# A rotary embedding on one core: the first piece's row 0 is stored by a DMA of its own

## The chip, the cores and the metric

The kernel runs on 1 core of one Trainium2 chip. The metric is device time in microseconds; for a kernel the median of several runs is given. All times below that carry a place in the execution are counted from the start of the profiled span.

## The reference

```python
def setup_inputs():
    batch, seq_len, num_heads, head_dim = (8, 2048, 16, 64)
    return {'x': np.random.randn(batch, seq_len, num_heads, head_dim).astype(np.float32), 'cos': np.random.randn(seq_len, head_dim // 2).astype(np.float32), 'sin': np.random.randn(seq_len, head_dim // 2).astype(np.float32)}

def reference(x, cos, sin):
    x1 = x[..., :head_dim // 2].copy()
    x2 = x[..., head_dim // 2:].copy()
    cos = cos[None, :, None, :].copy()
    sin = sin[None, :, None, :].copy()
    out1 = x1 * cos - x2 * sin
    out2 = x1 * sin + x2 * cos
    return np.concatenate([out1, out2], axis=-1).astype(np.float32)
```

Each head's 64 numbers are two halves of 32; the output is the input times cos plus the input with its halves exchanged times (-sin, sin). The input x is 67.1 MB of float32, the output as much, cos and sin 0.26 MB each. So at least 134.7 MB go through the DMA engines.

## The kernel before

A sequence position of one batch is a row of 16 x 64 floats, 4096 bytes. The 2048 positions of a batch are laid out with 16 consecutive ones to a partition (J = 16), and a piece is 8 of these rows (R = 8) on all 128 partitions: 32,768 contiguous bytes a partition, 4 MB in all. There are 16 pieces, two to a batch. They live in one SBUF tile, `buf`, with five slots (NBUF = 5); piece p uses slot p % 5 and is changed in place.

For a stretch of rows of a piece, `rotate` issues: a product v = x with exchanged halves times the signed sin (VectorE, L80), a product x = x times cos in place (VectorE, L93), and the sum x = x + v in place (GpSimd, L99). In the last piece a part of the sum is done on VectorE (L87 and L96). `in_order` keeps VectorE's instructions in program order. Most pieces are two stretches of four rows, so two additions of 128x4096. Piece 0 is cut finer: rows 0 to 2, 2 to 4, and 4 to 8, so that its three additions on GpSimd are of 128x2048, 128x2048 and 128x4096.

All loads are issued by SyncE (SP) at L52 (cos and sin at L101 and L103), all stores by ScalarE (ACT) at L55. Piece 0 is loaded in three DMAs (1, 1 and 2 MB), every other piece in one of 4 MB. Pieces 0 to 4 are loaded at the start; the load of piece p + 5 is issued when the store of piece p has landed, as it goes into the same slot. Pieces 0 to 14 leave by one store of 4 MB each, the last piece by three of 2, 1 and 1 MB. A store waits for the additions of its rows. ScalarE does nothing else besides three small copies of sin and cos into PSUM at the start.

Every DMA is spread over 16 DMA engines, 8 partitions to each, and each partition's contiguous bytes are one packet: a 4 MB load or store is 8 packets of 32,768 bytes on each engine, and one of 4 bytes that signals its completion. Loads and stores are two queues (q1 and q10 in the profile) that share the same 16 engines. The compiler gives the DMAs eight completion semaphores in rotation, and a DMA whose semaphore is in use by an earlier one waits for that one to land.

Of the kernel before, what the change touches and what calls it, by code (L numbers as in the profile page):

```python
# [1 line left out]

# [4 lines left out]


@with_exitstack  # L10
def kernel(
    ctx: ExitStack,
    tc: tile.TileContext,
    x: bass.AP,
    cos: bass.AP,
    sin: bass.AP,
    out: bass.AP,
):
    nc = tc.nc
    f32 = mybir.dt.float32  # L20

    B, S, H, D = x.shape
    Dh = D // 2
    P = nc.NUM_PARTITIONS
    J = S // P
    R = 8
    C = 4
    HALVES = J // R
    NP = B * HALVES
    NBUF = 5  # L30

    const_pool = ctx.enter_context(tc.tile_pool(name="rope_const", bufs=1))
    io_pool = ctx.enter_context(tc.tile_pool(name="rope_io", bufs=1))
    tmp_pool = ctx.enter_context(tc.tile_pool(name="rope_tmp", bufs=2))
    ps_pool = ctx.enter_context(tc.tile_pool(name="rope_ps", bufs=1, space=bass.MemoryType.PSUM))
    psv_pool = ctx.enter_context(tc.tile_pool(name="rope_psv", bufs=1, space=bass.MemoryType.PSUM))

    sin_f = const_pool.tile([P, J, Dh], f32)
    cos_f = const_pool.tile([P, J, Dh], f32)
    sin_p = ps_pool.tile([P, J, D], f32)  # L40
    cos_p = ps_pool.tile([P, J, Dh], f32)
    buf = io_pool.tile([P, NBUF, R, H, D], f32)

    def rows(t, p, r0, r1):
        b, j0 = p // HALVES, (p % HALVES) * R
        return t[b].rearrange("(p j) h d -> p j (h d)", j=J)[:, j0 + r0 : j0 + r1, :].rearrange("p j f -> p (j f)")

    def flat(t):
        return t.rearrange("p j h d -> p (j h d)")

    def load(p, r0=0, r1=R):
        nc.sync.dma_start(out=flat(buf[:, p % NBUF, r0:r1, :, :]), in_=rows(x, p, r0, r1))  # L52

    def store(p, r0=0, r1=R):
        nc.scalar.dma_start(out=rows(out, p, r0, r1), in_=flat(buf[:, p % NBUF, r0:r1, :, :]))  # L55

    order = []

    def in_order(op):
        if order:  # L60
            tc.add_manual_dep(
                op.ins,
                order[-1].ins.name,
                mybir.DependencyInfo(mybir.DependencyClass.NoSync, mybir.DependencyReason.DATA),
                reason="order of the vector engine",
            )
        order.append(op)

    def rotate(p, r0, r1, on_vector=0):
        n = r1 - r0  # L70
        j0 = (p % HALVES) * R + r0
        js = slice(j0, j0 + n)
        xt = buf[:, p % NBUF, r0:r1, :, :]
        rev = xt.rearrange("p j h (e d) -> p j h e d", e=2)[:, :, :, ::-1, :]
        sin_b = sin_p[:, js, :].rearrange("p j (e d) -> p j e d", e=2).unsqueeze(2).to_broadcast([P, n, H, 2, Dh])
        cos_b = cos_p[:, js, :].unsqueeze(2).to_broadcast([P, n, 2 * H, Dh])
        m = n - on_vector
        if m:
            v = tmp_pool.tile([P, C, H, D], f32)
            in_order(nc.vector.tensor_mul(  # L80
                out=v[:, 0:m, :, :].rearrange("p j h (e d) -> p j h e d", e=2),
                in0=rev[:, 0:m, :, :, :],
                in1=sin_b[:, 0:m, :, :, :],
            ))
        if on_vector:
            w = psv_pool.tile([P, 2, H, D], f32)
            in_order(nc.vector.tensor_mul(  # L87
                out=w[:, 0:on_vector, :, :].rearrange("p j h (e d) -> p j h e d", e=2),
                in0=rev[:, m:n, :, :, :],
                in1=sin_b[:, m:n, :, :, :],  # L90
            ))
        xw = xt.rearrange("p j h (e d) -> p j (h e) d", d=Dh)
        in_order(nc.vector.tensor_mul(out=xw, in0=xw, in1=cos_b))  # L93
        if on_vector:
            xa = flat(xt[:, m:n, :, :])
            in_order(nc.vector.tensor_add(out=xa, in0=xa, in1=flat(w[:, 0:on_vector, :, :])))  # L96
        if m:
            xa = flat(xt[:, 0:m, :, :])
            nc.gpsimd.tensor_add(out=xa, in0=xa, in1=flat(v[:, 0:m, :, :]))  # L99

    nc.sync.dma_start(out=sin_f, in_=sin.rearrange("(p j) d -> p j d", j=J))  # L101
    load(0, 0, 2)
    nc.sync.dma_start(out=cos_f, in_=cos.rearrange("(p j) d -> p j d", j=J))  # L103
    load(0, 2, 4)
    load(0, 4, R)
    for p in range(1, NBUF):
        load(p)
    nc.scalar.copy(out=sin_p[:, :, Dh:D], in_=sin_f)  # L108
    nc.scalar.mul(out=sin_p[:, :, 0:Dh], in_=sin_f, mul=-1.0)  # L109
    nc.scalar.copy(out=cos_p, in_=cos_f)  # L110
    for p in range(NP):
        if p == 0:
            rotate(p, 0, 2)
            rotate(p, 2, 4)
            rotate(p, 4, 8)
            store(p)
        elif p == NP - 1:
            rotate(p, 0, 4, 1)
            store(p, 0, 4)
            rotate(p, 4, 6, 1)  # L120
            store(p, 4, 6)
            rotate(p, 6, 8, 2)
            store(p, 6, 8)
        else:
            rotate(p, 0, 4)
            rotate(p, 4, 8)
            store(p)
        if p + NBUF < NP:
            load(p + NBUF)


# [1 line left out]
_INS = ['x', 'cos', 'sin']  # L133
_OUTS = [((8, 2048, 16, 64), 'float32')]


# [23 lines left out]
```

## Time and profile before

| | us |
|---|---|
| median of 3 runs | 318.33 |
| lowest and highest | 318.25, 318.38 |
| the profiled execution | 318.49 |
| its span, first to last instruction | 316.7 |

| engine | busy us | share of the span |
|---|---|---|
| VectorE | 287.5 | 91% |
| GpSimd | 274.8 | 87% |
| ScalarE | 3.1 | 1% |

| DMA | what it is |
|---|---|
| read from HBM | 67.63 MB |
| written to HBM | 67.11 MB |
| mean over the span | 425 GB/s |

The profiled execution's time is 1.8 us longer than its span: that is what lies before the first and behind the last instruction. A row of the table by stretches that is used below gives, for a stretch of the span, how long each engine was busy, and for the DMA packets that *started* in it the share of the 16 engines' time that they took and their bytes over the stretch's length. The trace has, besides, a record of every DMA packet: queue, start, duration, size.

### The profile page before, as it was taken

How to read it: one execution, taken by the hardware profiler on the slowest of the kernel's cores; microseconds unless marked ns; L12 is line 12 of the kernel's file. 1: busy time of each engine (PE TensorE's matmuls, PEld its weight loads, DVE VectorE, ACT ScalarE, POOL GpSimd, SP SyncE). 2: the span in 40 equal slices, each digit the busy share in tenths (PEclk: the TensorE clock that was granted, in tenths of full speed). 3: DMA queues.
4: the chain of work that ended last, by engine and by line, in shares of the span. 5: the costliest groups of instructions: out<-in, count | busy, mean ns of one | idle time of the engine just before them, and what ended most of it. 6: DMA issues, size and time to landing. Idle time of an engine off the chain costs nothing.

```text
span 316.7 us, 272 instructions
## 1 busy us (share of the span) xinstructions
DVE 287.5 (91%) x73; ACT 3.1 (1%) x4; POOL 274.8 (87%) x37
## 2 busy tenths in 40 slices
DVE  2999999999999999999999999799697997979960
ACT  3000000000000000000000000000000000000000
POOL 0659999999999999999999999989969899797900
DMA  7999999999999999999999999999999999999997
GB/s 301 460 430 447 348 464 426 435 451 410 459 401 464 397 464 397 464 414 447 435 426 459 401 464 397 464 398 459 410 451 435 426 451 410 455 406 460 406 428 300
DMA packets 5474, 134.76 MB, mean 425 GB/s; under 512 B 608, under 2 KB 608, under 8 KB 864
## 3 DMA queue, kind: packets, MB, share of 16 engines
q1 hardware_dynamic: 2880, 67.63, 50.0%
q10 hardware_dynamic: 2592, 67.11, 49.1%
q14 instruction: 2, 0.02, 0.0%
HBM read 67.63 MB, written 67.11 MB: 425 GB/s over the span
## 4 chain that ended last, share of the span: by engine, by line
POOL 39%; DMA 32%; DVE 21%; issue 3%; SPq 0%; POOLq 0%; DVEq 0%
POOL buf L99 39%; DMA buf<-in_x_dram 22%; DMA out_dram<-buf 11%; DVE buf L93 10%; DVE v L80 8%; DVE buf L96 1%; DVE w L87 1%; SPq L101 0%; POOLq L99 0%; DVEq L80 0%; SPq L52 0%
## 5 line engine op out<-in xcount | busy, mean ns | idle before, releaser
L99 POOL TENSOR_TENSOR buf<-buf,v 128x4096 f32<-128x4096 f32 (+3 forms) x33 | 274.6, 8335 | 26.2 <-DVE buf L93 25.8
L80 DVE TENSOR_TENSOR v<-buf,sin_p 128x4096 f32<-128x4096 f32 (+3 forms) x33 | 137.3, 4161 | 17.3 <-DMA buf<-in_x_dram 15.7
L93 DVE TENSOR_TENSOR buf<-buf,cos_p 128x4096 f32<-128x4096 f32 (+1 forms) x34 | 141.8, 4170 | 1.2
L96 DVE TENSOR_TENSOR buf<-buf,w 128x1024 f32<-128x1024 f32 (+1 forms) x3 | 4.7, 1575 | 0.1
L87 DVE TENSOR_TENSOR w<-buf,sin_p 128x1024 f32<-128x1024 f32 (+1 forms) x3 | 4.7, 1579 | 0.0
L108 ACT ACT_TABLE_LOAD x1 | 1.3, 1283 | 0.7 <-PEq L144 0.7
L110 ACT COPY cos_p<-cos_f 128x512 f32<-128x512 f32 x1 | 0.6, 590 | 2.1 <-DMA cos_f<-in_cos_dram 2.1
L108 ACT COPY sin_p<-sin_f 128x512 f32<-128x512 f32 x1 | 0.6, 589 | 1.4 <-DMA sin_f<-in_sin_dram 1.4
L109 ACT ACTIVATE sin_p<-sin_f 128x512 f32<-128x512 f32 x1 | 0.6, 601 | 0.0
L144 POOL MEMSET const-float32-0.0<- 128x1 f32 x1 | 0.1, 98 | 0.2 <-issue 0.2
L144 POOL MEMSET const-bfloat16-1.0<- 128x1 bf16 x1 | 0.1, 101 | 0.0
L144 POOL MEMSET const-uint8-127<- 128x1 uint8 x1 | 0.1, 101 | 0.0
L144 POOL MEMSET const-float32-1.0<- 128x1 f32 x1 | 0.1, 98 | 0.0
## 6 DMA issues: line engine op xcount, KB each, us to landing
buf<-in_x_dram SPq DMA_DIRECT2D x15, 4096.0 KB, 31.4
out_dram<-buf ACTq DMA_DIRECT2D x15, 4096.0 KB, 31.4
buf<-in_x_dram SPq DMA_DIRECT2D x2, 1024.0 KB, 6.0
buf<-in_x_dram SPq DMA_DIRECT2D x1, 2048.0 KB, 11.5
out_dram<-buf ACTq DMA_DIRECT2D x1, 2048.0 KB, 11.9
out_dram<-buf ACTq DMA_DIRECT2D x2, 1024.0 KB, 10.8
sin_f<-in_sin_dram SPq DMA_DIRECT2D x1, 256.0 KB, 2.7
cos_f<-in_cos_dram SPq DMA_DIRECT2D x1, 256.0 KB, 5.1
```

The costliest lines, as they stand in the source:

```text
L80: in_order(nc.vector.tensor_mul(out=v[:, 0:m, :, :].rearrange("p j h (e d) -> p j h e d", e=2), in0=rev[:, 0:m, :, :, :], in1=sin_b[:, 0:m ...
L87: in_order(nc.vector.tensor_mul(out=w[:, 0:on_vector, :, :].rearrange("p j h (e d) -> p j h e d", e=2), in0=rev[:, m:n, :, :, :], in1=sin_ ...
L93: in_order(nc.vector.tensor_mul(out=xw, in0=xw, in1=cos_b))
L96: in_order(nc.vector.tensor_add(out=xa, in0=xa, in1=flat(w[:, 0:on_vector, :, :])))
L99: nc.gpsimd.tensor_add(out=xa, in0=xa, in1=flat(v[:, 0:m, :, :]))
L108: nc.scalar.copy(out=sin_p[:, :, Dh:D], in_=sin_f)
L109: nc.scalar.mul(out=sin_p[:, :, 0:Dh], in_=sin_f, mul=-1.0)
L110: nc.scalar.copy(out=cos_p, in_=cos_f)
L144: nc = _bacc.Bacc("TRN2", target_bir_lowering=False, num_devices=1)
```

## The change

The store of piece 0 is cut in two. Row 0 (4096 bytes a partition, 512 KB in all) is stored by a DMA of its own that is issued behind the first `rotate`, which has added rows 0 and 1. Rows 1 to 8 (28,672 bytes a partition, 3.5 MB) follow where the store of the whole piece was.

```diff
     for p in range(NP):
         if p == 0:
             rotate(p, 0, 2)
+            store(p, 0, 1)
             rotate(p, 2, 4)
             rotate(p, 4, 8)
-            store(p)
+            store(p, 1, 8)
         elif p == NP - 1:
             rotate(p, 0, 4, 1)
             store(p, 0, 4)
```

The computation, the loads and all other stores are as they were. There is one DMA more on ScalarE's queue, 19 rather than 18.

## The prediction

> **What bounds the kernel now.** I read the share of each engine first, then the DMA rows, then the chain of waits, and then a table by stretches.
>
> ```profile
> DVE 287.5 (91%) x73; ACT 3.1 (1%) x4; POOL 274.8 (87%) x37
> DMA  7999999999999999999999999999999999999997
> GB/s 301 460 430 447 348 464 426 435 451 410 459 401 464 397 464 397 464 414 447 435 426 459 401 464 397 464 398 459 410 451 435 426 451 410 455 406 460 406 428 300
> q1 hardware_dynamic: 2880, 67.63, 50.0%
> q10 hardware_dynamic: 2592, 67.11, 49.1%
> POOL 39%; DMA 32%; DVE 21%; issue 3%; SPq 0%; POOLq 0%; DVEq 0%
> ```
>
> The chain names GpSimd first, but it only walks back along one possible path. The DMA rows say what cannot be shortened: the 16 engines are busy in every slice but the first and the last, and the packets of the two queues took 50.0 + 49.1 = 99.1% of the span. The rates jump between slices because a slice is credited with packets that start in it, and a round of 16 packets of 32 KB is half a MB.
>
> The packet records give the account. A packet of 2, 8, 16 and 32 KB takes 0.084, 0.309, 0.611 and 1.213 us: nearly 0.008 us and 27.2 GB/s. One engine has 240 packets of 32 KB, 16 of 16 KB, 32 of 8 KB and 16 of 2 KB: 291.1 + 9.8 + 9.9 + 1.3 = 312.1 us. The first packet starts at 1.74 and the last ends at 315.42, 313.7 us apart. So each engine loses only 1.6 us between its first and last packet, and I looked for where:
>
> ```profile
> 33.90:35.10 1.20, 1.20 (x1) 0.00 (x0) 1.20 (x1) 1.00 1.01 437
> 35.10:36.60 1.50, 1.50 (x1) 0.00 (x0) 1.50 (x1) 1.00 1.03 350
> 36.60:38.35 1.75, 1.72 (x2) 0.00 (x0) 1.75 (x1) 1.00 0.97 300
> 38.35:39.50 1.15, 1.15 (x1) 0.00 (x0) 1.15 (x1) 1.00 1.05 456
> 39.50:40.70 1.20, 1.20 (x1) 0.00 (x0) 1.20 (x1) 1.00 1.01 437
> ```
>
> Each row holds one packet of 32 KB on each engine (rate x length is 0.525 MB, 16 packets), so share x length is its mean duration: 1.21, then 1.545 and 1.70, then 1.21 again. The first two slow ones are loads; the next is the first packet of the first store. By the packet records the two cost 0.85 us an engine with their gaps (0.74 to 1.01 on the 16). They follow on this:
>
> ```profile
> 10.90 9.04 POOL L99 TENSOR_TENSOR buf<-buf,v 128x2048 f32<-128x2048 f32 x2 [10.46 <-DVE buf L93]
> ...
> 24.41 17.69 POOL L99 TENSOR_TENSOR buf<-buf,v 128x4096 f32<-128x4096 f32 x2 [4.46 <-DVE buf L93]
> 28.70 4.42 DVE L93 TENSOR_TENSOR buf<-buf,cos_p 128x4096 f32<-128x4096 f32 x1
> 33.31 0.38 ACTq L55 DMA_DIRECT2D out_dram<-buf  x1
> ```
>
> So: store queue empty, loads streaming, the first store is issued at 33.31, 1.8 us later the loads slow, and 5.1 us after the issue the store's first packet starts. From there on the queues alternate packet by packet, neither runs empty until the loads end at 281.4, and no later store or load issue shows such a loss. I call it the start-up of the store queue. The kernel is bound by the DMA engines' packet time, start-ups included.
>
> **The change, part by part.**
>
> *Bytes and packets.* The bytes are the same; so the early row gains nothing by itself: the engines are full with loads at that time, and 512 KB moved forward push loads back by as much. On each engine 8 packets of 32 KB become 8 of 4 and 8 of 28 KB. From 0.008 us and 27.2 GB/s: 0.159 + 1.062 - 1.213 = 0.008 us, by 8 is 0.064; with one more completion packet (0.009 us in the records) +0.07 us. All of it is on the bound.
>
> *The store queue starts twice.* The early store is issued when the first addition ends: GpSimd starts at 10.90 and its two additions of 128x2048 take 4.5 us each, so at about 15.46. By the same delays as before its first packet starts at about 15.46 + 5.1 = 20.6. Eight packets of 4 KB alternate with loads, (0.159 + 1.213) x 8 = 11.0, so it is done at about 31.6. The next store's descriptors are there at 33.31 + 1.8 = 35.1. So the queue is empty for about 3.5 us with loads streaming, as it was before its first start, and starts again. The trace does not show a second start. Bounds: 0 if the loss belongs to the first use, 0.85 us if to each start; below nothing if the small first store makes both cheaper (a rival). Nearest row: at 210.41 one engine had a packet of 8 KB of its instruction queue, empty for 200 us, between loads and stores; the load behind it took 1.747 rather than 1.213 us, 0.53 lost (in the store-only stretch, at 285.32, only 0.09). That is a queue joining a stream of loads after the program's start, with a loss of the same order. I take 0.85.
>
> *The Trainium skill.* "DMA: Bandwidth & Descriptors", Rules for kernel authors, asks for DMAs of 1 MiB and more, and its Anatomy section puts a fixed cost of about 2.0 us on each (fitted on the GpSimd path). By that the sum would be 318.33 + 2.0 = 320.3. The trace speaks against it in a stream: loads 1 and 2 land at 23.35 and 33.05, 9.70 us apart, which is 8 x 1.213.
>
> *Other engines.* The loss at about 17 to 20 us and the 4 KB packets fall on load 1, which lands at 23.35 + 0.85 + 2 x 0.159 = 24.5 rather than 23.35. VectorE starts on it at 24.25 now, and a landing reaches its waiter 0.45 us later (store 0 landed at 56.91, load 5 is issued at 57.35): it starts at about 24.95, 0.7 late. GpSimd then is 0.7 late for piece 1, and store 1 is issued at about 51.9 instead of 51.17. Its descriptors are there 1.8 us later, at 53.7; the store queue needs them when the 3.5 MB store's eight rounds are over, at 38.4 + 8 x (1.062 + 1.213) = 56.6: 2.9 us of cover. Without it loads 3 and 4 would fill the engines, and a third start-up would be the loss. At the end, the last store is issued at 306.2, and its packets start only when the one before it is done, at 312.97: 4.9 us of cover behind the 1.8 of an issue. So lateness of compute costs nothing.
>
> *Queues and semaphores.* On ScalarE's queue the early store stands ahead of the 3.5 MB store, which waits longer anyway. The semaphore rotation shifts by one: loads 3 and 4 now wait for piece 0's first two loads (landed at 5.7 and 8.8) rather than for sin and cos (3.0 and 6.4); 10 MB are queued ahead of them. Load 5 waits for both stores; the early one lands some 24 us before the other. Nothing.
>
> Sum on the profiled execution: 318.49 + 0.07 + 0.85 = 319.41; it stands 0.16 above the median of the runs, so 319.25 for the median.
>
> **Rivals.**
>
> *A: the loss is paid once* (first use of the store queue, or nearly nothing for packets of 4 KB). Then 318.33 + 0.07 = 318.40, with partial losses up to 318.9. For it: no later issue shows a loss; but the queue was never empty at one. The same comes out if the early store were in fact held until the later one's addition.
>
> *B: faster.* The loss belongs to the first packet ever stored and grows with its size. Then the early row pays 0.85 x 4/32 = 0.11 and the big store none: 318.33 + 0.07 + 0.11 - 0.85 = 317.66. It counts as faster if the two starts together cost under 0.14 us (318.33 + 0.07 + 0.14 - 0.85 = 317.69, 0.2% below). For it: the 0.85 is 70% of a 32 KB packet's time, as if part of that packet were read before the loads ahead of it are written. Against: the instruction queue's packet was only 8 KB and cost 0.53.
>
> *C: each 4 KB packet costs the load behind it 0.53 us,* like that 8 KB one. Then 8 x 0.53 = 4.2 more: 318.33 + 0.07 + 0.85 + 4.2 = 323.5. Against: the 4-byte completion packets stand between loads at 211.4 and the loads behind them take 1.213.
>
> *D: a DMA's latency in the stream.* The first load, 256 KB, is issued at 0.74 and landed 2.7 us after (its row says 2.7), of which 8 x 0.084 is data: 2.0 us. Were that idle for the added store: 320.3. Same figure as the skill's rule; the loads that land 9.70 apart speak against it.
>
> **How the numbers follow.** Start-up paid twice 46%; A 27%; B 16%; C 6%; D 5%. Within 0.2% (0.64 us, about what a measurement of this kernel can tell from no change) lie 317.69 to 318.97. Slower: the main case, C and D, 0.57. Faster: B, which lies close to the bound, less 0.02 for what may fall short of it, 0.14. Same: A and those 0.02, 0.29. The likeliest case's own range is 319.0 to 319.5 (0.85 spread by the 0.74 to 1.01 of the engines). To hold 8 in 10 the range takes in A and B: 317.6 to 319.6; C and D are left out.
>
> **What would show it.** In the rows by stretches and the packet records of the changed kernel: two loads of about 1.5 to 1.7 us on each engine at 17 to 20 us, and two more at 35 to 38.4; eight 4 KB packets of 0.16 between loads of 1.213; VectorE idle for some 0.7 us before piece 1; everything from 60 us on as before, but 0.9 later at the end. Wrong if one of the two pairs is missing (A or B), if the loads between 20 and 31 us are longer than 1.213 (C), or if the end moves by something that is in neither.

## The result, and the profile after

| | before | after |
|---|---|---|
| median us | 318.53 (318.25 to 319.73, 6 runs) | 323.58 (322.43 to 325.35, 6 runs) |
| ratio, with its 95% interval | | 1.0157 [1.0137, 1.0177] |
| profiled execution, us | 318.49 | 323.54 |
| its span, us | 316.7 | 321.8 |

The change costs 1.6%, 5.05 us on the profiled executions. The forecast was 319.25 with a range of 317.6 to 319.6: the direction was right, the size was not. The intervals here and below leave out runs more than 1.5% above the fastest of their kernel, which for a kernel that spreads widely is its slow half; so the spread of all runs is given beside them.

The page of the changed kernel, in the lines that were shown of the one before:

```profile
DVE 287.3 (89%) x73; ACT 3.1 (1%) x4; POOL 274.7 (85%) x37
DMA  7999999999999999999999999999999999998995
GB/s 309 469 403 448 379 427 432 456 407 424 428 428 444 424 428 440 420 432 436 407 452 420 428 436 424 428 437 428 420 420 444 432 428 416 452 407 376 399 420 249
q1 hardware_dynamic: 2880, 67.63, 49.7%
q10 hardware_dynamic: 2736, 67.11, 48.5%
DMA 50%; DVE 26%; POOL 19%; SPq 1%; issue 1%; DVEq 0%; POOLq 0%
```

VectorE and GpSimd work as long as before (287.3 and 274.7 us). The DMA engines still look full, 98.2% of a longer span, and the bytes are the same: the same work takes the same engines longer. Only the slices near the end (376, 399) show a hole. A table by stretches says where the rate falls; its columns are the stretch, its length, the busy time of VectorE, ScalarE and GpSimd, the clock, and the DMA share and GB/s of the packets that start in it. Before:

```profile
33.00:46.00 13.00, 12.77 (x4) 0.00 (x0) 12.84 (x3) 1.00 1.00 403
46.00:90.00 44.00, 43.39 (x11) 0.00 (x0) 43.70 (x6) 1.00 1.00 430
90.00:290.00 200.00, 188.87 (x45) 0.00 (x0) 191.00 (x22) 1.00 1.00 433
297.00:302.00 5.00, 4.90 (x4) 0.00 (x0) 4.23 (x2) 1.00 0.97 419
```

After:

```profile
33.00:46.00 13.00, 12.78 (x4) 0.00 (x0) 12.55 (x3) 1.00 1.00 413
46.00:90.00 44.00, 43.52 (x11) 0.00 (x0) 43.51 (x6) 1.00 1.01 432
90.00:290.00 200.00, 182.05 (x42) 0.00 (x0) 184.12 (x22) 1.00 1.00 430
297.00:302.00 5.00, 4.97 (x4) 0.00 (x0) 2.91 (x2) 1.00 0.81 347
```

The start of the big store is no dearer than before (413 against 403; the edges of short stretches can move such a rate by some per cent). Far from the change, from 90 to 290 us, the share is 1.00 in both, and yet 430 GB/s come out instead of 433: packets take longer while they count as busy. And from 297 to 302 us a fifth of the DMA time is empty. The waits say who pays. Before, then after:

```profile
POOL buf L99 <- DVE buf L93: 25.8, 15, 10.5
DVE v L80 <- DMA buf<-in_x_dram: 15.7, 7, 6.1
```

```profile
POOL buf L99 <- DVE buf L93: 33.1, 15, 10.4
DVE v L80 <- DMA buf<-in_x_dram: 23.8, 10, 6.1
```

VectorE waits 8.1 us longer for loads. A mean over 16 engines hides the rest, because a DMA has landed only when the slowest engine is done. The packet records carry no engine number, but each packet starts where the one ahead of it on its engine ends, so they can be strung together engine by engine. "Loss" below is the time of a packet beyond the usual one for its size (0.159, 0.309, 0.611, 1.062, 1.213 us for 4, 8, 16, 28, 32 KB) plus the gap ahead of it. Where several engines end at the same moment the strings can be swapped, so the means hold better than the figure of a single engine:

```
us lost on each of the 16 engines, after (mean before in brackets)
14 to 33 us   (0.01)  0.15 to 0.40, mean 0.30    the 4 KB packets' start-up
33 to 46      (0.85)  0.50 to 0.83, mean 0.63    the big store's start-up
24 to 33              0 on all                   seven or so 4 KB packets between loads
46 to 290     (0.06)  0.7 to 0.9 on 8 engines; 1.7 to 5.8 on the other 8
297 to 302    (0.00)  2.5 to 3.0 on the first 8; 0 to 1.7 on the others
last packet  (315.4)  318.2 on 13 engines, 319.9, 320.1 and 320.5 on three
```

So half of the engines fall behind, by up to 5.8 us, and the last load lands at 290.2 instead of 282.7. The end of the kernel then looks like this (start, duration, instruction). Before, then after:

```profile
283.16 3.35 DVE L80 TENSOR_TENSOR v<-buf,sin_p 128x3072 f32<-128x3072 f32 x1 [1.68 <-DMA buf<-in_x_dram]
...
290.52 16.04 ACTq L55 DMA_DIRECT2D out_dram<-buf  x4
```

```profile
290.63 3.35 DVE L80 TENSOR_TENSOR v<-buf,sin_p 128x3072 f32<-128x3072 f32 x1 [2.31 <-DMA buf<-in_x_dram]
...
297.66 16.36 ACTq L55 DMA_DIRECT2D out_dram<-buf  x4
299.61 1.22 DVE L96 TENSOR_TENSOR buf<-buf,w 128x1024 f32<-128x1024 f32 x1
```

The last piece's first product started at 283.16 before and starts at 290.63. The store of piece 14, at 290.52 before, is issued at 297.66, when the 8 engines that had lost little have stored all there was: their hole of 2.5 to 3.0 us. The engines that lost most have none, and the last packet ends 5.1 us later than before.

### The profile page after: what moved, and what is told of

Its sections match the earlier page's. It is cut to its first block, busy times and chain, and to the rows that moved or that the text cites. A ratio compares the mean times of both kernels' runs of the same rounds, so it can differ in the third digit from the quotient of the medians.

```text
span 321.8 us, 276 instructions
## 1 busy us (share of the span) xinstructions
DVE 287.3 (89%) x73; ACT 3.1 (1%) x4; POOL 274.7 (85%) x37
## 4 chain that ended last, share of the span: by engine, by line
DMA 50%; DVE 26%; POOL 19%; SPq 1%; issue 1%; DVEq 0%; POOLq 0%
DMA buf<-in_x_dram 30%; DMA out_dram<-buf 21%; POOL buf L99 19%; DVE buf L93 12%; DVE v L80 11%; DVE buf L96 1%; DVE w L87 1%; SPq L52 0%; SPq L103 0%; SPq L101 0%; DVEq L80 0%; POOLq L99 0%
```

## The experiments

**First batch: is it the cut, the second start, or engines that fall out of step?** In the kernel before, mostly all 16 engines carry a load packet or all a store packet at one moment; in the changed kernel, at 45 us, 9 carry loads and 7 stores. That was the first theory ("step"). The edits of the first three experiments are shown against the changed kernel, which differs from the kernel before by the early row alone.

`e1_late_split`:

```diff
             rotate(p, 0, 2)
-            store(p, 0, 1)
             rotate(p, 2, 4)
             rotate(p, 4, 8)
+            store(p, 0, 1)
             store(p, 1, 8)
```

> The store of piece 0 is cut into the same two DMAs, but both are issued behind the last addition of piece 0, at about 33.3 us. Theory 'step': what costs is that the 16 DMA engines fall out of step (at one moment some carry a load packet and others a store packet), which the second start of the store queue brought about; with one start of the queue they all take the store's first packet after the same load, stay in step, and the time is that of before plus the 0.07 us of added packets: 318.3 to 318.9. Rival 'cut': the packets of 4 KB and 28 KB, the added DMA or the shifted rotation of semaphores cost it: 322 to 324, as in the changed kernel. Rival 'starts': the store queue's start-ups themselves cost, one more of them costs 0.6 to 0.9: 318.4 here.

Measured 320.93 (318.14 to 323.48, 10 runs), ratio 1.0039 [1.0004, 1.0075].

`e2_row0_later`:

```diff
             rotate(p, 0, 2)
-            store(p, 0, 1)
             rotate(p, 2, 4)
+            store(p, 0, 1)
             rotate(p, 4, 8)
             store(p, 1, 8)
```

> Row 0 is stored by itself behind the second addition (issue at about 20.0 us instead of 15.4), so that its eight 4 KB packets, one per load packet, last until about 36 and the next store's descriptors come at about 35.1, before the queue is empty. One start, early. 'Step': 318.3 to 319.2 if the engines take their first store packet after the same load (16 to 0 at any moment), 322 to 324 if the one start splits them too; the packet records tell which, and time and split must go together. 'Cut': 322 to 324 whatever the split. 'Starts': 318.4 whatever the split.

Measured 320.20 (319.41 to 323.93, 10 runs), ratio 1.0069 [1.0032, 1.0107]. Both expectations rest on an edit that did nothing: where the store stands in the program does not hold it back. It waits for the addition of its own rows and for nothing else, and it was issued at 16.35 in the first and 15.40 in the second, as in the changed kernel (15.39). On each engine the two have the changed kernel's instructions in its order, so they are repeats of it, and as such they told most: in these two, one and the same program takes 318.14 to 323.93 us. In the profile of the first (319.90, span 318.1, of which 0.9 is a late beginning) 0.08 us an engine is lost between 90 and 290 us; in that of the second (323.76) 3.6 us.

`e3_three`:

```diff
             rotate(p, 0, 2)
-            store(p, 0, 1)
+            store(p, 0, 2)
             rotate(p, 2, 4)
+            store(p, 2, 4)
             rotate(p, 4, 8)
-            store(p, 1, 8)
+            store(p, 4, 8)
```

> Piece 0 leaves as three stores, rows 0 to 2, 2 to 4 and 4 to 8, each issued behind its own addition (about 15.4, 20.0, 33.3 us): packets of 8, 8 and 16 KB, the queue starts once, early, and has work until the third arrives at about 35. 'Step': 318.3 to 319.2 if the engines stay 16 to 0, 322 to 324 if they split. 'Cut' (more DMAs and more short packets than in the changed kernel): 323 or more. 'Starts': 318.5.

Measured 318.63 (318.20 to 319.69, 10 runs), ratio 0.9999 [0.9982, 1.0015]. More DMAs, shorter packets and an early start cost nothing. And its engines were out of step, 6 with one kind of packet and 10 with the other more often than any other way (38% of the time from 60 to 290 us), with 0.21 us lost from 90 to 290: "step" falls too.

`e4_skew16`, on the kernel before:

```diff
+    for i in range(1):
+        spare = tmp_pool.tile([P, C, H, D], f32, name="v")
+        nc.sync.dma_start(
+            out=flat(spare)[0:8, :],
+            in_=x[0].rearrange("(p j) h d -> p (j h d)", j=J)[0:8, i * C * H * D : (i + 1) * C * H * D],
+        )
     nc.sync.dma_start(out=sin_f, in_=sin.rearrange("(p j) d -> p j d", j=J))
```

> The kernel before, with one load of 16 KB on each of 8 partitions put ahead of all others; its data are not used. If it runs on 8 of the 16 engines, these are 0.61 us (half a 32 KB packet) behind the other 8 from then on, with the stores exactly as before. 'Step': the two halves are out of step when stores begin, and the time rises by more than the 0.61 us of data: 320 to 324, with landings that spread more from load to load. 'Cut' and 'starts': nothing that they name is changed, at most +0.61: 318.3 to 319.0.

Measured 320.85 (319.99 to 321.85, 10 runs), ratio 1.0054 [1.0033, 1.0075]. The time lies in the range of "step", for another reason: ahead of 14 us the profile loses about 1.4 us an engine more than the kernel before. From 50 to 260 us the engines are out of step in nearly nine tenths of the time (at least 3 of them with the other kind of packet), and between 90 and 290 us they lose 0.07. A time that fits is not yet a mechanism.

What separates the profiles that lose from those that do not came out of the records: the time from the end of a load DMA to the end of the next store DMA on the same engine, called the distance from here on. In rounds of 2.42 us (a load and a store packet) it is 7.3 us on all engines of the kernel before, 4.8 on all 16 of `e1_late_split`, 9.7 and 12.1 in `e3_three`. In the changed kernel it is 4.8 on 9 engines, and 2.4 on 7, which are among the 8 that fall behind; in `e2_row0_later` 2.4 on 12.

**Second batch: set that distance without an early store.** The two queues of an engine take turns, packet by packet. If a DMA's completion packet takes a turn of its queue like any other packet, one load cut into more DMAs lets the store queue send one packet more for each added completion, and each extra turn should move the distance by a round, 2.42 us. `g1_load4_in3`, on the kernel before:

```diff
-    for p in range(1, NBUF):
+    def load_part(p, a, b):
+        nc.sync.dma_start(out=flat(buf[:, p % NBUF, :, :, :])[a:b], in_=rows(x, p, 0, R)[a:b])
+
+    for p in range(1, NBUF - 1):
         load(p)
+    load_part(NBUF - 1, 0, 96)
+    load_part(NBUF - 1, 96, 112)
+    load_part(NBUF - 1, 112, 128)
```

> No early store: the kernel before, with the load of piece 4 issued as three DMAs, on partitions 0 to 96, 96 to 112 and 112 to 128: the same bytes and packets, but two more completion packets in the load queue on each engine, each of which takes a load turn. Theory 'distance': what costs is how soon a store DMA ends behind a load DMA on an engine. It is 7.3 us on all engines in the kernel before (no loss), 4.8 on all in the undisturbed profile of the first experiment (no loss), 9.7 and 12.1 with three stores (no loss), but 2.4 on 7 of 16 engines of the changed kernel and on 12 of the second experiment, which lose 2 to 6 us. Two more load turns move 7.3 to 2.4 on every engine from about 70 us on, so the time rises by 3 to 6 us: 321 to 324. Rival 'split' (engines out of step): they stay in step, 318.3 to 318.8. Rival 'second start': there is none, 318.3 to 318.8.

Measured 334.40 (333.40 to 335.02, 4 runs), ratio 1.0493 [1.0471, 1.0515].

`g2_load4_in2` has the cuts (0, 112), (112, 128):

> The same with two DMAs, on partitions 0 to 112 and 112 to 128: one more load turn, the distance goes from 7.3 to 4.8. 'Distance': no loss, 318.2 to 318.9. If any cut of the load costs, 320 or more. 'Split' and 'second start': 318.3 to 318.8.

Measured 324.33 (322.64 to 324.98, 4 runs), ratio 1.0166 [1.0131, 1.0201].

`g4_load4_in4` has (0, 80), (80, 96), (96, 112), (112, 128):

> The kernel before with the load of piece 4 as four DMAs (partitions 0 to 80, 80 to 96, 96 to 112, 112 to 128): three more load turns, distance about 0: a load DMA and a store DMA end together on each engine. 'Distance', if what hurts is that both queues begin a new DMA within one or two rounds: 321 or more. 'Split' and 'second start': 318.3 to 318.8.

Measured 330.76 (330.07 to 331.50, 4 runs), ratio 1.0382 [1.0361, 1.0403].

By their times the loads in three and in two missed the ranges of the theory they were to test, and none of the three times decides anything, because the edit brought a cost of its own: with the load cut by partitions the engines lost 9.4, 5.9 and 11.7 us (in three, two, four) between 46 and 90 us, while these loads ran. Why such a cut costs was not looked into. Behind 90 us, where the edited load is past and the distance is what is left of it, the profiles are clear: at 2.4 (in three) 4.85 us lost up to 290, at 4.8 (in two) 0.06, at 0 (in four) 0.06. The distances are those that 2, 1 and 3 added completion packets should give.

`g3_repair` put the same three cuts on the changed kernel's second store:

```diff
-            store(p, 1, 8)
+            for a, b in ((0, 96), (96, 112), (112, 128)):
+                nc.scalar.dma_start(out=rows(out, p, 1, 8)[a:b], in_=flat(buf[:, p % NBUF, 1:8, :, :])[a:b])
```

> The changed kernel, early row and second start included, with the store of rows 1 to 8 issued as three DMAs on partitions 0 to 96, 96 to 112 and 112 to 128: two more store turns, which put 2.4 and 4.8 at 7.3 and 9.7. 'Distance': the loss is gone, 318.2 to 319.2, and the spread of the runs with it. 'Second start' or 'split': 320 to 325, as in the changed kernel.

Measured 322.33 (321.02 to 323.76, 4 runs), ratio 1.0118 [1.0083, 1.0153]: missed. The distance did go to 7.3 and 9.7 and the loss from 90 to 290 us to 0.24, but 0.8 us were lost on the mean between 46 and 90, up to 1.6 on one engine. No verdict on the time.

**Third batch: the same with small packets, no cut.** `h1_turns2`, on the kernel before; `h2_turns3` has 32 in place of 16:

```diff
+    spare = const_pool.tile([P, J * Dh], f32)
...
     for p in range(1, NBUF):
         load(p)
+    nc.sync.dma_start(out=spare[0:16, :], in_=sin.rearrange("(p j) d -> p (j d)", j=J)[0:16, :])
```

> The kernel before with one more load of 2 KB on each of 16 partitions (32 KB in all, data not used) behind the load of piece 4: one small packet and one completion packet in the load queue of every engine, so two more load turns. No early store, no cut of a load or store, one start. Theory 'distance 2.4': from about 70 us on every engine ends its store DMA 2.4 us behind a load DMA instead of 7.3, as the cut of the load in three did from 90 us on (4.85 us lost an engine from 90 to 290 us, against 0.06 in the kernel before): 321 to 324. Rival 'the cut itself' (other partitions to an engine): 318.3 to 318.9. Rivals 'split' and 'second start': 318.3 to 318.9.

Measured 323.90 (320.65 to 324.05, 4 runs), ratio 1.0141 [1.0091, 1.0191].

> The same load on 32 partitions: two small packets and a completion packet, three more load turns, so the distance is 0 instead of 2.4; 32 KB more bytes than in its neighbour. 'Distance 2.4': the cut of the load in four had 0 and lost 0.06 us an engine from 90 to 290 us, so 318.3 to 319.0. If small loads or lateness of the load queue cost: as much as the neighbour or more.

Measured 319.17 (318.59 to 319.42 in nine runs, and one of 334.19), ratio 1.0008 [0.9993, 1.0022]. The median is 0.2 above the range given. This is the cleanest pair: 32 KB more cost about 5 us (one run in four only 2), 64 KB more cost nothing that can be told. The stretch from 90 to 290 us, first with two more turns, then with three:

```profile
90.00:290.00 200.00, 181.69 (x42) 0.00 (x0) 183.78 (x22) 1.00 1.00 425
```

```profile
90.00:290.00 200.00, 184.66 (x43) 0.00 (x0) 186.88 (x22) 1.00 1.00 433
```

A share of 1.00 in both, 425 and 433 GB/s: the loss sits inside the packets' durations. By the records it is 3.82 and 0.11 us an engine.

`h3_repair_tiny`, on the changed kernel:

```diff
             store(p, 1, 8)
+            nc.scalar.dma_start(out=rows(out, p, 0, 1)[0:16], in_=flat(buf[:, p % NBUF, 0:1, :, :])[0:16])
```

> The changed kernel with a store of row 0 on 16 partitions again (64 KB, the same data to the same place) between the early row and the store of rows 1 to 8: two more store turns, the same partitions to an engine otherwise. 'Distance 2.4': 2.4 and 4.8 become 7.3 and 9.7, the loss after 60 us is gone: 318.2 to 319.3 in all runs. 'Second start' or 'split': 320 to 325, as in the changed kernel beside it.

Measured 323.40 (320.00 to 324.36, 4 runs), ratio 1.0121 [1.0056, 1.0187]: missed. It too was issued as soon as it could be, at 30.71, ahead of the store of rows 1 to 8 (33.10), so its turns were spent before the start that matters. The distances stayed 2.4 (9 engines) and 4.8, and the loss with them, 3.63.

`h4_after_again` is the changed kernel, unedited:

> The changed kernel once more, on the chip of the other three. It gave 322.4 to 325.4 in 6 runs, and the same instruction streams under the first two experiments' names 318.1 to 323.9 in 20. 'Distance 2.4': its runs spread between 318.2 (no engine at 2.4) and 325 (most at 2.4), and its profile's loss goes with the number of engines at 2.4.

Measured 322.15 (320.61 to 324.25, 4 runs), ratio 1.0115 [1.0066, 1.0164]. Its profile: 12 engines at 2.4, 4.11 lost.

**Fourth batch: the changed kernel with the distance moved, and the addresses.** `i1_after_turns4` is the changed kernel with the line of `h1_turns2`, on 48 partitions.

> The changed kernel, early row and second start of the store queue included, with one more load of 2 KB on each of 48 partitions (96 KB, data not used) behind the load of piece 4: four more load turns on each engine, which move a distance of 2.4 to 7.3 before the load's end and one of 4.8 to 4.9 before it (12.1 and 14.5 after the one before). The tiny store of the third batch did not do that: it went out before the second start and moved nothing. 'Distance 2.4': the loss after 90 us falls from 1.8 to 4.1 us an engine to under 0.4, and the time to 318.4 to 319.6. 'Second start' or 'split', whose events are all still there: 320 to 325.

Measured 319.89 (318.72 to 321.02 in eleven runs, and one of 329.63), ratio 1.0036 [1.0023, 1.0049].

```profile
90.00:290.00 200.00, 184.41 (x43) 0.00 (x0) 186.59 (x22) 1.00 1.00 433
```

433 GB/s are back (430 in the changed kernel). The early row, the second start and 96 KB more are all there, and the loss from 90 to 290 us is 0.07. Where the distance went was not as expected: 1.3 and 2.6 at piece 2, then 0 on nearly all engines. The median is 0.3 above the range given for "distance" and 0.1 below that of its rivals, and four of the eleven runs took 320.06 to 321.02; only the profiled execution, 318.98, shows where its time went. So the times alone say that most of the cost is gone, not that all of it is.

`i2_turns2_swapped` is `h1_turns2` with the two halves of each batch stored in each other's place, so that its output is not the reference's:

```diff
-        nc.scalar.dma_start(out=rows(out, p, r0, r1), in_=flat(buf[:, p % NBUF, r0:r1, :, :]))
+        nc.scalar.dma_start(out=rows(out, p ^ 1, r0, r1), in_=flat(buf[:, p % NBUF, r0:r1, :, :]))
```

> The kernel with two more load turns (distance 2.4, 323.9 us), with the stores of the two halves of each batch exchanged (piece p is written where piece p xor 1 belongs), so all timing but the addresses written is the same. If the loss at 2.4 comes of which HBM addresses are read and written at the same time, it changes by more than a third (from 3.8 us an engine between 90 and 290 us) and the time with it: under 321.5 or over 326. If it comes of the two queues' turns alone, it stays: 322 to 325.

Measured 324.40 (320.61 to 325.00, 4 runs), ratio 1.0156 [1.0106, 1.0206], loss 3.37. So it does not come of which half is written while which is read.

All profiles together:

```
                   engines at 2.4   other engines at   us lost an engine, 90 to 290
before                   0               7.3               0.06
e4_skew16                0               7.3               0.07
e1_late_split            0               4.8               0.08
g2_load4_in2             0               4.8               0.06
g4_load4_in4             0               0                 0.06
h2_turns3                0               0                 0.11
i1_after_turns4          0               0                 0.07
e3_three                 0           9.7, 12.1             0.21
g3_repair                0           7.3, 9.7              0.24
after                    7               4.8               1.77
h3_repair_tiny           9               4.8               3.63
e2_row0_later           12               4.8, 5.1          3.61
h4_after_again          12               4.8, 5.1          4.11
i2_turns2_swapped       15               5.0               3.37
h1_turns2               16                                 3.82
g1_load4_in3            16                                 4.85
```

The counts tell kernels apart, not engines. In `after` eight of the nine engines at 4.8 lose 0.3 to 0.6 us. But in `e2_row0_later`, `h3_repair_tiny`, `h4_after_again` and `i2_turns2_swapped` the engines at 4.8 to 5.1 lose 2.2 to 4.6 us, as much as those at 2.4, while 16 engines at 4.8 with none at 2.4 lose 0.08 (`e1_late_split`). So an engine's own distance does not settle what it loses; a kernel loses between 90 and 290 us where some of its engines stand at 2.4. Nor is the loss spread evenly over the packets: in the six profiles with 9 or more engines at 2.4, the first three packets of each load carry 2.9 to 4.3 us of the 3.4 to 4.9.

None of the kernels was faster than the one before; `e3_three` is its equal.

**Why the changed kernel comes to 2.4.** Its two stores of piece 0 are issued here:

```profile
15.39 0.37 ACTq L55 DMA_DIRECT2D out_dram<-buf  x1
...
33.24 0.34 ACTq L55 DMA_DIRECT2D out_dram<-buf  x1
```

Two engines at the second start, from the packet records (start, L load, S store, 28 for 28 KB, a dot for a completion packet, in brackets ns beyond the usual):

```
33.02:L 34.23:L. 34.23:L 35.44:L(+232) 36.88:S28 37.94:L(+492) 39.64:S28 40.70:L
33.00:L 34.21:L. 34.22:L 35.43:L 36.64:L(+665) 38.51:S28 39.57:L 40.78:S28 41.84:L
```

On the first, two packets of load 3 go ahead of the first 28 KB store packet, on the second three. In the kernel before it is four on every engine: load 3 begins at 32.70 to 33.04 there and at 34.13 to 34.56 here, about one packet later. Where no turns were added, engines with four are at 7.3, with three at 4.8, with two at 2.4: in the profiles of before, `e1_late_split` (three on all), after (two on 7, three on 9), `e2_row0_later` (two on 12, three on 4) and, but for five engines, `h4_after_again`. The early row's packets and start-up push load 3 back by about a packet, while the big store's issue, set by GpSimd, stays at 33.2. Whether two or three loads go first is then a matter of tenths of a microsecond, and differs between engines and between executions. That would account for 318.14 to 325.35 us in the 30 runs of this one program (four of them were profiled), half of them at 322.17 or above, against 318.25 to 320.62 in 74 runs of the kernel before.

## Why the prediction was wrong, by its own steps

- *The bound.* Right: the DMA engines' packet time, start-ups included. The packets' durations came out as worked out, 0.159 and 1.062 us.
- *The early store's course.* Right: issued at 15.39 (15.46 forecast), first packets at 19.4 to 20.9 (20.6), done at 29.3 to 30.7 (31.6), the queue empty for some 4 to 6 us (the next store is issued at 33.24, and its descriptors are there 1.8 later by the forecast's own reckoning), then a second start with slow loads.
- *The second start costs 0.85.* Mis-sized. The two starts cost 0.30 + 0.63 in the profile after, 0.18 + 0.59 in `e1_late_split`, 0.24 + 0.79 in `e2_row0_later`, against 0.85 for one before: the term is -0.1 to +0.2. The forecast's own rival A, the loss paid once, was nearer (318.40), and the program's best runs (318.14 and 318.17) fit it.
- *The rest "as before".* This is the step that failed. The prediction checked that both queues always have work and that late compute has cover, and took it that then only bytes and packets count. It wrote that the early row pushes loads back "by as much" and did not ask what that does to where loads stand relative to stores. They moved by one or two rounds, for good, and with engines at one of these places packets take longer: 1.8 to 4.1 us an engine from 90 to 290 us in the three profiles of this program that have engines there, 1.8 on the mean and up to 5.1 on one engine in the profile of the changed kernel. The forecast put that term at nothing.
- *"Lateness of compute costs nothing", with 4.9 us of cover at the end.* It covers the 0.9 us that was expected. The last load landed 7.5 us later, which is more than the cover, and the engines that had kept up ran dry.
- *Rival C* gave 323.5, almost the measured time, by a mechanism that the trace refutes: between 24 and 33 us the loads behind 4 KB packets lose nothing. The Trainium skill's fixed cost for each DMA ("DMA: Bandwidth & Descriptors", Anatomy of one DMA), about 2 us by a formula that it fits on the GpSimd path, is not seen either in these DMAs of SyncE and ScalarE: `e3_three` has two DMAs more than the kernel before and its ratio is 0.9999.

Shown: that between 90 and 290 us the profiles with engines at 2.4 lose 1.8 us or more and the others at most 0.24 (16 profiles), that two more turns bring the loss to the kernel before, where a third takes it away again, and that moving the distance takes it from the profile of the changed one. Not shown: what happens in the DMA engines at that distance, why the first three packets of a load pay for it, and why engines at 4.8 pay beside them. One kind of address conflict was tried and is not it. The single runs of 334.19 and 329.63 are unexplained too.

## What to carry to other kernels

When loads and stores share DMA engines that are never idle, an added DMA can cost more than its bytes and its start: it can shift for good where the ends of loads and stores fall relative to each other, and here one such place was slow. Work out that shift in packet turns, completion packets included, and repeat the measurement: a wide spread between runs of one program is a sign of it. A busy share of 1.00 doesn't show it; the rate and the packets' durations do.

## What the runs showed of the hardware that was not expected

- With 7 to 16 engines on which a store DMA ends one round (2.4 us) behind a load DMA: 1.8 to 4.9 us lost an engine in 200 us, mostly in the first three packets of a load, and with 9 to 15 such engines the others lose as much. With none there, at 0, 4.8 and 7.3 us: 0.06 to 0.11.
- A 4-byte completion packet takes a whole turn of its queue: one small DMA of one packet moved the distance from 7.3 to 2.4, one of two packets to 0.
- Where a store stands in the program did not hold it back, as ScalarE had no other work in between: issued at 16.35 and 15.40 us for two later places, at 15.39 for the first.
- The same 4 MB load as DMAs on 112 and 16 partitions instead of 128 cost 5.9 us an engine between 46 and 90 us (one profile); the reason is open.
